# A decoder layer in float32 on one core: seven block products per weight group, in another order, in fewer PSUM banks, with weights split 1024 wide

## The chip, the cores and the metric

The kernel runs on one core of a Trainium2 chip, as one launch. The metric is the device time of that core in microseconds (us). The engines are named as the profile names them: PE (TensorE matmul), PEld (its weight loads), DVE (VectorE), ACT (ScalarE), POOL (GpSimd), SP (SyncE, which issues nearly all DMAs).

## The reference

One decoder layer on 1024 tokens of width 1024, all in float32. The two feed-forward blocks (FFN1 and FFN2, inner width 2816) are where the change lies; the mixer between them isn't touched.

```python
def swiglu(h, w_gate, w_up, w_down):
    return (jax.nn.silu(h @ w_gate) * (h @ w_up)) @ w_down

h = modulate(rms_norm(x, ffn1_norm[l]), sh1, sc1)
x = x + 0.5 * g1[:, None, :] * swiglu(h, ffn1_w_gate[l], ffn1_w_up[l], ffn1_w_down[l])
...
h = modulate(rms_norm(x, ffn2_norm[l]), sh3, sc3)
x = x + 0.5 * g3[:, None, :] * swiglu(h, ffn2_w_gate[l], ffn2_w_up[l], ffn2_w_down[l])
```

## The kernel before, in words

**Matmuls in three pieces.** Each float32 operand is split into a high part (rounded to fp32r by an ACT cast) and a low part (the rest, by a DVE subtraction). `mm3` issues three matmuls of 512 columns for one product of 128 by 128 by 512: high by high, high by low, low by high. The weights are split on the chip too: `Weights.pump` takes a raw tile of 1 MB that SP has loaded (`rawp`, two buffers), casts 512 or 1024 columns of it on ACT and subtracts on DVE, into a tile named w of 1024 columns (a granule). `ws.take()` gives the next granule to PE, `ws.free()` gives its slot back and calls `pump`, so that each split is emitted where a slot was freed. The instructions of DVE and of ACT are issued in the order in which the program emits them.

**Seven products in place of eight.** The 2816 inner columns are 11 groups of 256. In most groups (fa2 to fa10 in FFN1, fb1 to fb10 in FFN2) gate and up are each computed as a product of two-by-two blocks with seven block products instead of eight: A11, A12, A22 and the sums S1 to S4 of blocks of the activations, against B11, B12, B22 and sums of blocks of the weights (t1 to t4 in the code). One block product of one side (g for gate, u for up) is 12 matmuls into one PSUM bank. `seven(name, between, place, kept, then)` does first all seven products of g, then all seven of u. Its table names the bank of each: A11 and A12 accumulate in A, S1 and S4 in C, S2 in B, S3 in D, A22 in E. The sums over the banks are made after the products: per side one ACT copy (of A11) and five DVE additions, each of 128x512 with one operand in PSUM. The pool `mm_ps` has six banks; a new tile takes the bank that was released longest ago, and PE waits until the readers of the tile that had it are done.

**Weight sums.** Each raw tile of a seven-product group holds B11, B21, B22, B12 of gate or up, 512 columns each. `combine` (L168, L169) and `split_done` (L177, L179) form the sums with four POOL operations of 128x512 per raw tile, eight per group. A granule is two blocks that stand one after the other in the list SEVEN, so it is split in two halves of 512, and belongs to products n and n+1 of one side.

**Down projections.** `down7` does the same with seven products for four groups at a time (fad0, fad1, fbd0, fbd1), over two pairs of output tiles p; their results update x by a DVE operation. `down2` is the plain down projection of one group: 16 tiles of 6 matmuls, each followed by an update of x on DVE. For group fb0 it runs inside fb1: `seven("fb1", lambda: down2(...), 0, ...)` calls it as `between` after the first product of g. In the program's names its PSUM tiles are fb0d, with d from 0 to 7 for the two token halves.

**Around it.** In FFN1, work that the mixer needs later (names bb, cl, bl, rot, tab, ph and the like) is emitted in small steps between the matmuls by `clock.tick`. `keep`, `keep_sums` and `keep_last` store the products' results to DRAM; `fetch` brings them back for `down7`. Names in the profile: fa6gC is bank C of group fa6's gate side, fa6gt, fa6gu its SBUF tiles, h and h1S (h3 and h3S in FFN2) the split activations and their sums.

Of the kernel before, what the change touches and what calls it, by code (L numbers as in the profile page):

```python
# [13 lines left out]
F32 = mybir.dt.float32  # L14
# [3 lines left out]
ALU = mybir.AluOpType  # L18
# [102 lines left out]
class Weights:  # L121
# [5 lines left out]
    SEVEN = (0, "t1", "t2", "t3", 3, "t4", 2)  # L127
    SECOND = (0, "t2", 3, "t3", "t1", "t4", 2)

    def __init__(self, engines, srcs, granules, raw_bufs):  # L130
        self.V, self.A, self.SP, self.G = engines
        self.srcs, self.granules, self.raw_bufs = srcs, granules, raw_bufs
        self.left = [0] * len(srcs)
        self.combined = {j for pair in granules for j, c in pair if isinstance(c, str)}
        for pair in granules:
            for j, _ in pair:
                self.left[j] += 1
# [3 lines left out]
        self.slots = deque()  # L141

# [9 lines left out]
    def load(self, upto):  # L152
        while len(self.raws) < min(upto, len(self.srcs)):
# [3 lines left out]
            self.raws.append(r[:].rearrange("p a b -> p (a b)"))  # L157
# [6 lines left out]
    def combine(self, j):  # L164

        f = self.sums_pool.tile([P, HALF], F32, tag="sums", name=f"sums{j}")[:]
        r = [self.raws[j][:, c * HALF : (c + 1) * HALF] for c in range(4)]
        self.G.tensor_tensor(out=f, in0=r[2], in1=r[1], op=ALU.subtract)  # L168
        self.G.tensor_tensor(out=r[1], in0=r[1], in1=r[0], op=ALU.subtract)  # L169
        self.sums[j] = {"t1": r[1], "t2": r[0], "t3": f, "t4": r[0]}  # L170

    def split_done(self, j, c):

        if j in self.combined and c in (0, "t2"):
            s, r = self.sums[j], self.raws[j][:, :HALF]
            if c == 0:
                self.G.tensor_tensor(out=r, in0=s["t3"], in1=r, op=ALU.add)  # L177
            else:
                self.G.tensor_tensor(out=r, in0=self.chunk(j, 3), in1=r, op=ALU.subtract)  # L179

    def chunk(self, j, c):
        if isinstance(c, int):
            return self.raws[j][:, c * 512 : (c + 1) * 512]
        return self.sums[j][c]

    def pump(self):
        while self.slots and len(self.tiles) < len(self.granules):
            i = len(self.tiles)
            pair = self.granules[i]
            (j0, c0), (j1, c1) = pair  # L190
            if self.sums_pool is None and (j0 in self.combined or j1 in self.combined):
                return
            self.load(max(j0, j1) + 1)
            for j, c in pair:
                if j in self.combined and j not in self.sums:
                    self.combine(j)
# [3 lines left out]
            if j0 == j1 and isinstance(c0, int) and c1 == c0 + 1:  # L200
                parts = [(slice(0, 1024), self.raws[j0][:, c0 * 512 : (c0 + 2) * 512])]
            else:
                parts = [(slice(512 * q, 512 * q + 512), self.chunk(*c)) for q, c in enumerate(pair)]
# [6 lines left out]
            for j, _ in pair:  # L210
                self.left[j] -= 1
# [24 lines left out]
def hymba_layer(ctx: ExitStack, tc, x_d, xt_d, wm1_d, wmod_d, gu1_d, gs1_d, ds1_d, wl1_d, win_d, wout_d, glu_d, gu2_d, gs2_d, wd2_d, ds2_d, wl2_d, cols_d, cond_d, lam_d, bc_d, out_d):  # L236
# [49 lines left out]
    def plain(arrays):  # L286
        for a in arrays:
            granules.extend([[(len(srcs), 2 * q), (len(srcs), 2 * q + 1)] for q in range(2)])
            srcs.append(a)

    def stream(gu, gs, wd, ds, wl, m):
# [4 lines left out]
        for g in range(m, NGRP):  # L296
# [3 lines left out]
            seven = [(i, c) for i in (j, j + 1 + inner) for c in Weights.SEVEN]  # L300
            seven = [seven[i : i + 2] for i in range(0, 14, 2)]
            if inner:
                granules.extend(seven[:1] + [[(j + 1, 2 * q), (j + 1, 2 * q + 1)] for q in range(2)] + seven[1:])
            else:
                granules.extend(seven)
        for c in range(CHUNKS):
            for p in range(2):
                j = len(srcs)
                srcs.extend([ds[c, p, 0], ds[c, p, 1]])
                granules.extend([(j, s), (j + 1, s)] for s in Weights.SECOND)  # L310
# [338 lines left out]
    def seven(name, between, place=1, kept=None, then=None):  # L649


        a_tiles, gate_, taken = {}, {}, []

        for side in "gu":
            bank, res = {}, {}

            def add(dst, src, b):
                V.tensor_tensor(out=dst[:], in0=src[:], in1=bank[b][:], op=ALU.add)

            def out(h, fi, t):  # L660
                nm = f"{name}_{fi}_{h}"
                if side == "g":
                    A.activation(t[:], t[:], AF.Silu)
                    gate_[h, fi] = t
                elif kept is None:
                    V.tensor_tensor(out=t[:], in0=t[:], in1=gate_[h, fi][:], op=ALU.mult)
                    a_tiles[fi, h] = split_act(t[:], nm + "a")
                else:
                    keep(kept, f"A{h + 1}{fi + 1}", t[:], gate_[h, fi][:], ALU.mult, name, t[:])

            for n, (left, b) in enumerate(SEVEN):
                q = n + 7 * (side == "u")
                if q % 2 == 0:
                    taken = ws.take()
                opens = b not in bank
                if opens:
                    bank[b] = ps(f"{name}{side}{b}")
                for k in range(4):
                    while len(blocks[left]) <= k:
                        clock.step()  # L680
                    mm3(bank[b][:], taken[0], q % 2 * 4 + k, blocks[left][k], opens and k == 0, k == 3, more=not opens)
                nm = f"{name}{side}"
                if n == 0:
                    t1 = t2k(nm + "t1")
                    A.copy(t1[:], bank["A"][:])
                elif n == 2:
                    u2 = t2k(nm + "u2")
                    add(u2, t1, "B")
                elif n == 3:
                    u3 = t2k(nm + "u3")  # L690
                    add(u3, u2, "D")
                    add(t1, u3, "C")
                    out(1, 1, t1)
                elif n == 4 and side == "g":
                    t = pools["first"].tile([P, HALF], F32, tag="first", name=nm + "c11") if "first" in pools else acc_in_mov(nm + "c11")
                    A.activation(t[:], bank["A"][:], AF.Silu)
                    gate_[0, 0] = t
                elif n == 4:
                    t = gate_[0, 0]
                    if kept is None:  # L700
                        V.tensor_tensor(out=t[:], in0=t[:], in1=bank["A"][:], op=ALU.mult)
                        a_tiles[0, 0] = split_act(t[:], f"{name}_0_0a")
# [1196 lines left out]
```

## Time and profile before

| | |
|---|---|
| runs (us) | 1698.07, 1703.12, 1702.21; median 1702.21 |
| profiled execution: its span (the page gives no other time for it) | 1704.7 us, 20844 instructions |
| busy share of the span | PE 98%, DVE 74%, ACT 37%, POOL 22% |
| instructions | PE 7545 matmuls, DVE 1957, ACT 1064, POOL 297 |

The stages by the trace: a start up to 34 us; plain groups fa0 and fa1 up to 119.87; seven-product groups fa2 to fa10 up to about 460; down projections to 765; the mixer to 985; its output projection to 1055; FFN2 (fb0, fb1 to fb10, fbd0, fbd1 and a last plain down projection) to the end. A row of the trace's timeline gives start, duration, engine, line, operation, out<-in by name, count, and in brackets the idle time before it with what ended it. A helper records most operations, so that nearly all have line L112; the names tell them apart.

### The profile page before, as it was taken

To read this page: it belongs to the slowest core of one execution; us is meant where nothing else is said; L and a number is where in the kernel's file an instruction comes from. 1 tells how busy PE (TensorE), PEld (TensorE's weight loads), DVE (VectorE), ACT (ScalarE), POOL (GpSimd) and SP (SyncE) were. 2 spreads that over 40 slices of the span, in tenths; PEclk is the share of its full clock that TensorE was granted. 3 is DMA by queue.
4 is the path that set the end of the run, shared out by engine and by line. 5 is a ranking of instruction groups with operands and counts; after the bars stand their busy time and mean duration, and the time that the engine had idled before them with its cause. 6 is when DMAs were issued, how large, how long until landed. Compare 5 with 4: busy or idle time off the path is not lost.

```text
span 1704.7 us, 20844 instructions
## 1 busy us (share of the span) xinstructions
PE 1666.8 (98%) x7545; PEld 1369.9 (80%) x7545; DVE 1255.5 (74%) x1957; ACT 630.1 (37%) x1064; POOL 382.0 (22%) x297
## 2 busy tenths in 40 slices
PE   8999999999999999999999999999999999999997
PEld 5888877788878888788777878888888888888886
DVE  7897899998589978735555857957767667576655
ACT  6525323333354332331113415434344434322233
POOL 1012222242222412100000021122333223333212
PEclk9999999999999999999999999999999999999999
DMA  8544454544665448244654232324443343759212
GB/s 350 187 148 137 172 189 155 183 149 139 213 216 170 151 152 291 70 111 149 191 151 134 70 129 112 112 74 182 188 174 148 148 173 148 269 228 381 110 50 99
DMA packets 101625, 281.48 MB, mean 165 GB/s; under 512 B 19345, under 2 KB 34961, under 8 KB 90386
## 3 DMA queue, kind: packets, MB, share of 16 engines
q1 hardware_dynamic: 101522, 280.15, 46.6%
q8 instruction: 59, 0.97, 0.2%
q14 instruction: 44, 0.36, 0.1%
HBM read 195.69 MB, written 76.02 MB: 159 GB/s over the span
## 4 chain that ended last, share of the span: by engine, by line
PE 70%; DVE 8%; DMA 5%; issue 1%; ACT 0%; SPq 0%; POOL 0%; DVEq 0%; ACTq 0%; POOLq 0%
PE wo L112 4%; PE fald L112 3%; PE fb10d L112 2%; PE u L112 2%; PE fbd_1B L112 2%; PE fbd_0B L112 2%; DMA swz<-si 2%; DVE w L112 2%; PE fad_1B L112 2%; PE b L112 2%; PE fad_0B L112 1%; PE c L112 1%; PE fb0u L112 1%; PE fad_1C L112 1%; PE fbd_1C L112 1%; PE fbd_0C L112 1%
## 5 line engine op out<-in xcount | busy, mean ns | idle before, releaser
L112 ACT CAST w<-raw 128x512 fp32r<-128x512 f32 (+1 forms) x374 | 240.9, 677 | 497.7 <-issue 72.7
L112 DVE TENSOR_TENSOR w<-raw,w 128x512 fp32r<-128x512 f32 (+1 forms) x374 | 311.2, 851 | 101.2 <-ACT w L112 100.6
L177 POOL TENSOR_TENSOR raw<-sums,raw 128x512 f32<-128x512 f32 x54 | 81.6, 1511 | 420.9 <-DVE w L112 419.9
L168 POOL TENSOR_TENSOR sums<-raw 128x512 f32<-128x512 f32 x54 | 76.4, 1415 | 308.1 <-DMA raw<-in_ds 129.1
L179 POOL TENSOR_TENSOR raw<-raw 128x512 f32<-128x512 f32 x54 | 82.3, 1526 | 86.6 <-DVE w L112 86.0
L112 DVE CUSTOM_DVE_ANT_0 wm<-wm,cact 128x1024 f32<-128x1024 f32 x56 | 77.7, 1407 | 15.1 <-DMA wm<-in_wmod 15.0
L169 POOL TENSOR_TENSOR raw<-raw 128x512 f32<-128x512 f32 x54 | 85.2, 1577 | 4.2
L370 POOL TENSOR_TENSOR n3aq<-n3aq,n3aq 128x512 f32<-128x512 f32 x5 | 7.5, 1499 | 277.4 <-ACT n3aq L112 277.2
L112 DVE TENSOR_TENSOR w<-sums,w 128x512 fp32r<-128x512 f32 x54 | 54.9, 1029 | 3.4 <-ACT w L112 2.8
L112 PE MATMUL p<-h,w 128*128 128x512 f32 x192 | 49.4, 407 | 2.0 <-ACT h L112 1.5
L112 PE MATMUL wo<-oa,w 128*128 128x512 f32 x192 | 45.5, 391 | 2.1 <-ACT w L112 1.3
L112 PE MATMUL c<-h,w 128*128 128x512 f32 x192 | 47.1, 397 | 0.0
L112 PE MATMUL v<-h,w 128*128 128x512 f32 x192 | 46.9, 395 | 0.0
L112 PE MATMUL b<-h,w 128*128 128x512 f32 x192 | 45.6, 393 | 0.0
L112 PE MATMUL wo<-ob,w 128*128 128x512 f32 x192 | 45.2, 391 | 0.0
L112 PE MATMUL u<-h,w 128*128 128x512 f32 x192 | 44.8, 392 | 0.2 <-DVE h L112 0.2
L112 PEld LDWEIGHTS wo<-oa,w 128*128 128x128 f32 x192 | 35.8, 188 | 10.2 <-ACT w L112 1.7
L112 PEld LDWEIGHTS p<-h,w 128*128 128x128 f32 x192 | 35.7, 192 | 10.1 <-ACT h L112 2.0
L112 ACT CAST w<-sums 128x512 fp32r<-128x512 f32 x54 | 32.7, 619 | 28.8 <-PE fa10gE L112 2.5
L112 PEld LDWEIGHTS u<-h,w 128*128 128x128 f32 x192 | 35.7, 188 | 8.3 <-DVE h L112 0.6
L112 PEld LDWEIGHTS wo<-ob,w 128*128 128x128 f32 x192 | 35.8, 188 | 7.4
L112 PEld LDWEIGHTS c<-h,w 128*128 128x128 f32 x192 | 35.8, 190 | 7.2
(1579 smaller groups left out, 4039.8 us busy)
## 6 DMA issues: line engine op xcount, KB each, us to landing
raw<-in_gs SPq DMA_DIRECT2D x38, 1024.0 KB, 5.0
wm<-in_wmod SPq DMA_DIRECT2D x56, 512.0 KB, 5.2
raw<-in_ds SPq DMA_DIRECT2D x16, 1024.0 KB, 6.6
mw<-in_wm SPq DMA_DIRECT2D x8, 1024.0 KB, 8.4
raw<-in_win SPq DMA_DIRECT2D x8, 1024.0 KB, 5.5
raw<-in_gu SPq DMA_DIRECT2D x6, 1024.0 KB, 4.9
raw<-in_wl SPq DMA_DIRECT2D x5, 1024.0 KB, 6.7
xb<-in_xt SPq DMA_DIRECT2D x8, 512.0 KB, 6.4
```

The costliest lines, as they stand in the source:

```text
L112: r = getattr(self.engine, name)(*args, **kw)
L168: self.G.tensor_tensor(out=f, in0=r[2], in1=r[1], op=ALU.subtract)
L169: self.G.tensor_tensor(out=r[1], in0=r[1], in1=r[0], op=ALU.subtract)
L177: self.G.tensor_tensor(out=r, in0=s["t3"], in1=r, op=ALU.add)
L179: self.G.tensor_tensor(out=r, in0=self.chunk(j, 3), in1=r, op=ALU.subtract)
L370: nc.gpsimd.tensor_tensor(out=a, in0=a, in1=sq[:, :n], op=ALU.add)
```

## The change

The raw tiles are laid out otherwise by the host: of each group, raw tile j holds B11 and B12, raw tile k = j+1 holds B22 and B21, each block with its 512 gate columns and its 512 up columns side by side. A granule is now one block for gate and up, split by one ACT cast and one DVE subtraction of 1024 columns; seven granules a group, as before. POOL forms the sums with four operations of 128x1024 per group (L170, L171, L172 of the new kernel one after the other, once both raw tiles are there, and L191 after the granule t3 is split). The pool of sums has one buffer of 1024 columns in place of two of 512.

`seven` does each product for g and then for u. The order is now A11, S1, S2, A12, S3, S4, A22, and the banks are B, C, B, A, B, C, B: the products in B accumulate on one another and are read in between. Per side there are three ACT copies (t1, c1, u2) and three DVE additions; the last product is read straight from bank B. `between` runs after the first product of both sides, `then` (fetches for the next `down7`) once per product of both sides, and the storing of sums comes after the whole group. `down7` uses the same table.

```diff
+    def seven(j, k):
+        return [(j, 0, k), (j, "t1", k), (j, "t2", k), (k, 1, k), (j, "t3", k), (k, 0, k), (j, "t4", k)]
...
+    def chunk(self, j, c, k):
         if isinstance(c, int):
+            return self.raws[j][:, c, :]
+        if c == "t1":
+            f = self.sums[j] = self.sums_pool.tile([P, 1024], F32, tag="sums", name=f"sums{j}")
+            b11, b12, b22 = self.raws[j][:, 0, :], self.raws[j][:, 1, :], self.raws[k][:, 0, :]
+            self.G.tensor_tensor(out=f[:], in0=b22, in1=b12, op=ALU.subtract)
+            self.G.tensor_tensor(out=b12, in0=b12, in1=b11, op=ALU.subtract)
+            self.G.tensor_tensor(out=b11, in0=f[:], in1=b11, op=ALU.add)
+        return {"t1": self.raws[j][:, 1, :], "t2": self.raws[j][:, 0, :]}.get(c, self.sums[j][:])
...
-            for q, src in parts:
-                hi, lo = w[:, 0, q], w[:, 1, q]
-                self.A.copy(hi, src)
-                self.V.tensor_tensor(out=lo, in0=src, in1=hi.bitcast(F32), op=ALU.subtract)
-                self.split_done(*pair[q.start // HALF])
+            hi, lo = w[:, 0, :], w[:, 1, :]
+            self.A.copy(hi, src)
+            self.V.tensor_tensor(out=lo, in0=src, in1=hi.bitcast(F32), op=ALU.subtract)
+            if c == "t3":
+                f = self.sums[j][:]
+                self.G.tensor_tensor(out=f, in0=self.raws[k][:, 1, :], in1=self.raws[j][:, 0, :], op=ALU.subtract)
...
-    SEVEN = (("A11", "A"), ("S1", "C"), ("S2", "B"), ("S3", "D"), ("A12", "A"), ("A22", "E"), ("S4", "C"))
-    SECOND = (("A11", "A"), ("S2", "B"), ("A12", "A"), ("S3", "B"), ("S1", "C"), ("A22", "B"), ("S4", "C"))
+    SEVEN = (("A11", "B"), ("S1", "C"), ("S2", "B"), ("A12", "A"), ("S3", "B"), ("S4", "C"), ("A22", "B"))
...
+        for n, (left, b) in enumerate(SEVEN):
+            (w,) = ws.take()
+            for half, side in enumerate("gu"):
...
+                    mm3(bank[b, side][:], w, 4 * half + k, blocks[left][k], opens and k == 0, k == 3, more=not opens)
                 if n == 0:
+                    copied(t1, "B", side, "t1")
+                elif n == 1:
+                    copied(c1, "C", side, "c1")
                 elif n == 2:
+                    copied(u2, "B", side, "u2")
                 elif n == 3:
+                    add(t1, "A", side)
+                    out(side, 0, 0, t1[side], t1[side])
                 elif n == 4:
+                    add(c1, "B", side)
+                    out(side, 1, 1, c1[side], c1[side])
                 elif n == 5:
+                    add(u2, "C", side)
+                    out(side, 0, 1, u2[side], u2[side])
+                else:
+                    if side == "g":
+                        last = pools["first"].tile([P, HALF], F32, tag="first", name=f"{name}c21") if "first" in pools else acc_in_mov(f"{name}c21")
+                    out(side, 1, 0, bank["B", side], last)
+            ws.free()
+            if n == 0 and between is not None:
+                between()
+            if then is not None:
+                then(left)
...
-        ws.sums_pool = es.enter_context(tc.tile_pool(name="sums", bufs=2))
+        ws.sums_pool = es.enter_context(tc.tile_pool(name="sums", bufs=1))
...
-    seven("fb1", lambda: down2(a_prev, 2, "fb0", (0, 1)), 0, kept[1])
+    seven("fb1", lambda: down2(a_prev, 2, "fb0", (0, 1)), kept[1])
```

How the order of the instructions moves is shown at two places. The first is DVE in the middle of group fa6; w is a granule's low part, X a stored sum, bb, cl, clt and bl belong to the mixer's preparation. Before:

```order
L112 TENSOR_TENSOR bl_2812<-tab_1652,bb_2764 128x512
L112 TENSOR_TENSOR fa6uu_2778<-fa6ut_2704,fa6uB 128x512
L112 TENSOR_TENSOR w_2783<-raw_2573,w_2783 128x512 x2
L112 TENSOR_TENSOR fa6uu_2802<-fa6uu_2778,fa6uD 128x512
L112 TENSOR_TENSOR fa6ut_2704<-fa6uu_2802,fa6uC 128x512
L112 TENSOR_TENSOR fa6X<-fa6ut_2704,fa6gt_2523 128x512
L112 TENSOR_TENSOR fa6X<-fa6gc_2644,fa6uA 128x512
```

Changed:

```order
L112 TENSOR_TENSOR fa6gc_2496<-fa6gc_2496,fa6gB 128x512
L112 TENSOR_TENSOR bb_2655<-prm_2652,qq 128x128
L112 TENSOR_TENSOR bb_2656<-prm_2652,qq 128x128
L112 TENSOR_TENSOR bb_2654<-bb_2655,bb_2656 128x64 x2
L112 TENSOR_TENSOR cl_2661<-tab_1609,prm_2652 128x576
L112 TENSOR_TENSOR clt_2662<-tab_1610,prm_2652 128x576
L112 TENSOR_TENSOR fa6uc_2511<-fa6uc_2511,fa6uB 128x512
L112 TENSOR_TENSOR cl_2661<-cl_2661,clt_2662 128x576
L112 TENSOR_TENSOR fa6X<-fa6uc_2511,fa6gc_2496 128x512
L112 TENSOR_TENSOR w_2671<-raw_2517,w_2671 128x1024
```

Before, bank C is given back only by the second of two additions that stand behind the product S3 of the same side; in the change one addition stands behind each product, and bank B of g is given back by fa6gc's.

The second place is DVE in `down2` of group fb0, inside fb1; the rows x<-fb0d are the updates that give fb0d's banks back, h3S are pieces of split activations, w the splits for fb1's next products. Before:

```order
L112 SCALAR_TENSOR_TENSOR x_0_3915<-fb0d_0_8957,gate,x_0_3915 128x512
L112 SCALAR_TENSOR_TENSOR x_0_3915<-fb0d_0_8969,gate,x_0_3915 128x512
L112 TENSOR_TENSOR h3S_0_8944<-h3S_0_8944 128x512
L112 SCALAR_TENSOR_TENSOR x_1_3918<-fb0d_1_8977,gate,x_1_3918 128x512
L112 TENSOR_TENSOR h3S_1_8964<-h3S_1_8964 128x512
L112 TENSOR_TENSOR h3S_2_8984<-h3S_2_8984 128x512
L112 SCALAR_TENSOR_TENSOR x_1_3918<-fb0d_1_8989,gate,x_1_3918 128x512
L112 TENSOR_TENSOR h3S_3_9004<-h3S_3_9004 128x512
L112 SCALAR_TENSOR_TENSOR x_1_3919<-fb0d_1_8997,gate,x_1_3919 128x512
L112 SCALAR_TENSOR_TENSOR x_1_3919<-fb0d_1_9009,gate,x_1_3919 128x512
L112 TENSOR_TENSOR w_9017<-raw_8442,w_9017 128x512
L112 TENSOR_TENSOR w_9017<-sums_8713,w_9017 128x512
```

Changed:

```order
L112 SCALAR_TENSOR_TENSOR x_0_3723<-fb0d_0_8686,gate,x_0_3723 128x512
L112 TENSOR_TENSOR h3S_0_8655<-h3S_0_8655 128x512
L112 SCALAR_TENSOR_TENSOR x_0_3724<-fb0d_0_8694,gate,x_0_3724 128x512
L112 TENSOR_TENSOR h3S_1_8681<-h3S_1_8681 128x512
L112 TENSOR_TENSOR w_8671<-raw_8159,w_8671 128x1024
L112 TENSOR_TENSOR h3S_2_8701<-h3S_2_8701 128x512
L112 SCALAR_TENSOR_TENSOR x_0_3724<-fb0d_0_8706,gate,x_0_3724 128x512
L112 TENSOR_TENSOR h3S_3_8721<-h3S_3_8721 128x512
L112 SCALAR_TENSOR_TENSOR x_1_3727<-fb0d_1_8714,gate,x_1_3727 128x512
```

The split of the granule t1 (w_8671) stood behind the eighth update and stands now between the third and the fourth. In the built program fb0d's tiles take five PSUM banks in turn before (fb1's bank A of g holds the sixth), and four in the change (fb1's bank B of g and of u hold two): the fourth tile's bank is written again by the ninth tile before, and by the eighth in the change.

## Rows read from the trace of the kernel before

**Rows 1.** The page, part 1: busy time, share of the span, instructions.
```profile
PE 1666.8 (98%) x7545; PEld 1369.9 (80%) x7545; DVE 1255.5 (74%) x1957; ACT 630.1 (37%) x1064; POOL 382.0 (22%) x297
```
**Rows 2.** Busy time by stage: length, each engine (instructions), granted clock, DMA share, GB/s.
```profile
90.00:140.00 50.00, 49.07 (x217) 40.34 (x216) 45.82 (x108) 19.75 (x32) 12.71 (x41) 1.00 0.36 122
140.00:450.00 310.00, 305.62 (x1384) 249.11 (x1383) 262.19 (x399) 105.33 (x194) 92.28 (x61) 1.00 0.49 166
450.00:640.00 190.00, 186.43 (x818) 152.70 (x817) 159.73 (x219) 83.98 (x148) 52.37 (x34) 1.00 0.52 178
...
1055.00:1643.00 588.00, 588.00 (x2597) 486.88 (x2596) 416.62 (x587) 218.42 (x380) 162.76 (x110) 1.00 0.46 176
```
**Rows 3.** What PE waited for, 90 to 700 us: total, times, longest.
```profile
PE fa4gC L112 <- DVE fa4gt L112: 1.6, 1, 1.6
PE fa10uC L112 <- DVE fa10ut L112: 1.5, 1, 1.5
PE fad_0A L112 <- DVE w L112: 1.5, 2, 0.8
PE fa5gC L112 <- DVE fa5gt L112: 1.2, 1, 1.2
PE fa2gC L112 <- DVE fa2gt L112: 0.9, 1, 0.9
PE fa5uC L112 <- DVE fa5ut L112: 0.9, 1, 0.9
PE fa6gC L112 <- DVE fa6gt L112: 0.7, 1, 0.7
PE fad_0B L112 <- DVE fad_0u L112: 0.5, 1, 0.5
```
**Rows 4.** Timeline of PE in group fa6: two products in a row.
```profile
315.30 2.88 PE L112 MATMUL fa6uA<-h,w 128*128 128x512 f32 x12
318.02 2.88 PE L112 MATMUL fa6uE<-h,w 128*128 128x512 f32 x12
```
**Rows 5.** Groups by shape on DVE: busy, mean ns of one, idle before, releaser.
```profile
L112 DVE TENSOR_TENSOR w<-raw,w 128x512 fp32r<-128x512 f32 x324 | 249.2, 791 | 67.4 <-ACT w L112 67.0
L112 DVE TENSOR_TENSOR w<-raw,w 128x1024 fp32r<-128x1024 f32 x50 | 62.0, 1244 | 33.8 <-ACT w L112 33.6
```
**Rows 6.** Groups by shape on ACT: a granule's casts, and the copy of a bank.
```profile
L112 ACT CAST w<-raw 128x512 fp32r<-128x512 f32 x324 | 188.5, 619 | 376.5 <-issue 72.7 <-POOL raw L177 60.7 <-DMA raw<-in_ds 44.1
L112 ACT CAST w<-raw 128x1024 fp32r<-128x1024 f32 x50 | 52.3, 1049 | 121.2 <-PE v L112 31.0 <-PE fald L112 18.4 <-PE wo L112 15.0
L112 ACT COPY fa3gt<-fa3gA 128x512 f32<-128x512 f32 x1 | 0.6, 589 | 1.6 <-PE fa3gA L112 1.6
```
**Rows 7.** Timeline of POOL in group fa6.
```profile
318.37 1.62 POOL L169 TENSOR_TENSOR raw<-raw 128x512 f32<-128x512 f32 x1
319.96 1.27 POOL L177 TENSOR_TENSOR raw<-sums,raw 128x512 f32<-128x512 f32 x1
```
**Rows 8.** Timeline of DVE in the same stretch.
```profile
318.76 0.68 DVE L112 TENSOR_TENSOR fa6uu<-fa6uu,fa6uD 128x512 f32<-128x512 f32 x1
319.47 0.69 DVE L112 TENSOR_TENSOR fa6ut<-fa6uu,fa6uC 128x512 f32<-128x512 f32 x1
320.19 1.59 DVE L112 TENSOR_TENSOR fa6X<-fa6ut,fa6gt 128x512 f32<-128x512 f32 x1
```
**Rows 9.** Timeline of PE at the start of group fb1.
```profile
1088.32 2.88 PE L112 MATMUL fb1gA<-h,w 128*128 128x512 f32 x12
1091.04 5.60 PE L112 MATMUL fb0d<-fb_0a,w 128*128 128x512 f32 x24
1096.48 5.60 PE L112 MATMUL fb0d<-fb_1a,w 128*128 128x512 f32 x24
```
**Rows 10.** Timeline of POOL at the same place.
```profile
1096.51 1.30 POOL L168 TENSOR_TENSOR sums<-raw 128x512 f32<-128x512 f32 x1 [18.14 <-DMA raw<-in_gs]
1097.88 1.29 POOL L169 TENSOR_TENSOR raw<-raw 128x512 f32<-128x512 f32 x1
```
**Rows 11.** Timeline of DVE at the same place.
```profile
1102.77 1.40 DVE L112 SCALAR_TENSOR_TENSOR x<-fb0d,gate,x 128x512 f32<-128x512 f32 x2
1104.09 0.68 DVE L112 TENSOR_TENSOR w<-raw,w 128x512 fp32r<-128x512 f32 x1
```
**Rows 12.** Timeline of ACT in group fa2: first and last of 13 rows without a gap.
```profile
137.33 1.17 ACT L112 COPY rt<-ph 64x512 f32<-64x512 f32 x1
...
146.54 1.14 ACT L112 CAST w<-raw 128x512 fp32r<-128x512 f32 x2
```

More of the change, by code (lines that the diff above doesn't have):

```diff
@@ L133, in __init__ @@
         self.left = [0] * len(srcs)
[L134 to L137, printed above, removed]
+        for j, c, _ in granules:
+            self.left[j] += c != "t4"
         self.raws, self.tiles, self.sums, self.kinds = [], [], {}, []
@@ L188, in pump @@
             i = len(self.tiles)
-            pair = self.granules[i]
-            (j0, c0), (j1, c1) = pair
-            if self.sums_pool is None and (j0 in self.combined or j1 in self.combined):
+            j, c, k = self.granules[i]
+            if self.sums_pool is None and c == "t1":
                 return
[L193 to L196, printed above, removed]
+            self.load((k if c == "t1" else j) + 1)
+            src = self.chunk(j, c, k)
             pool = self.slots.popleft()
@@ L287, in plain @@
         for a in arrays:
-            granules.extend([[(len(srcs), 2 * q), (len(srcs), 2 * q + 1)] for q in range(2)])
+            granules.extend((len(srcs), q, None) for q in range(2))
             srcs.append(a)
@@ L644, in combos3 @@
             yield
-    SEVEN = (("A11", "A"), ("S1", "C"), ("S2", "B"), ("S3", "D"), ("A12", "A"), ("A22", "E"), ("S4", "C"))
-    SECOND = (("A11", "A"), ("S2", "B"), ("A12", "A"), ("S3", "B"), ("S1", "C"), ("A22", "B"), ("S4", "C"))
[L649 to L675, printed above, removed]
@@ L686, in seven @@
                 elif n == 2:
-                    u2 = t2k(nm + "u2")
-                    add(u2, t1, "B")
+                    copied(u2, "B", side, "u2")
                 elif n == 3:
[L690 to L697, printed above, removed]
-                elif n == 4:
[L699 to L702, printed above, removed]
-                    else:
-                        keep(kept, "A11", t[:], bank["A"][:], ALU.mult, name, t[:])
-                elif n == 5:
-                    add(u3, u3, "E")
-                    out(1, 0, u3)
-                    if side == "u" and kept is not None and kept.sums:
-                        keep_sums(kept, name)
-                elif n == 6:
-                    add(u2, u2, "C")
-                    out(0, 1, u2)
-                    if side == "u" and kept is not None and kept.sums:
-                        keep_last(kept, name)
@@ L721, in seven @@
+            ws.free()
[3 more added lines that the diff above has]
+                then(left)
+        if kept is not None and kept.sums:
+            keep_sums(kept, name)
+            keep_last(kept, name)
         return a_tiles
@@ L1432, in hymba_layer @@
             pools.pop("first")
-        seven(f"fa{g}", lambda: None, kept=kept[g], then=(lambda left: fetch_chunk(0, left)) if g == NGRP - 1 else None)
+        seven(f"fa{g}", kept=kept[g], then=(lambda left: fetch_chunk(0, left)) if g == NGRP - 1 else None)
     down7("fad0", lefts[0], 0, lambda left: fetch_chunk(1, left), lambda left: load_x(range(2), (1, 3)) if left == "A12" else None)
```

120 lines of the change are left out of this document (50 added, 70 removed).

## The prediction

> **What bounds the kernel now.** I read the busy shares first [rows 1]: PE is busy for 1666.8 of 1704.7 us, and the reader is to see that nothing else comes near: DVE 74%, ACT 37%, POOL 22%. The change issues the same matmuls, so work saved on DVE, ACT or POOL is worth only what PE waits for them. So the second view is busy time by stage, where PE's idle time is the stage's length less its PE time [rows 2]: 0.9 us in 90 to 140, 4.4 in 140 to 450, 3.6 in 450 to 640, nothing at all in 1055 to 1643, where FFN2's seven-product groups lie. The granted clock is 1.00 in all four, the 2.4 GHz level, so no clock is to be won there. The third view is what PE waited for [rows 3]. Eight entries, 8.8 us in all, which is the idle time of the three stages. This is the ceiling of the gain: 0.5% of the span.
>
> Six entries, 6.8 us, are of one kind: the product S4 wants to open bank C again, and the second DVE addition behind S3 hasn't yet read it. The other two, 2.0 us, lie in the down projection fad0: a weight split that came late, and one addition.
>
> The sum is made against the profiled execution, 1704.7 us; it lies 2.5 us above the median of the runs, 1702.2, and I carry the difference over to the median.
>
> **The engines beside PE.** Of DVE's additions, 76 go in the 19 groups (two per side) and 32 in the down projections: 108 at 0.68 us [rows 8], about 73 us. 378 splits of 512 become 189 of 1024, at 1.24 us each [rows 5] in place of two at 0.79 or more; some 65 us. ACT gets 108 copies at 0.59, 64 us, and 189 casts at 1.05 in place of 378 at 0.62, 36 us less [rows 6]. POOL does 108 operations of twice the size, for about the same time. I count all of this at nothing: it lies beside matmuls, and DVE, the fullest, had 262 us of 310 filled in its worst stage [rows 2]. If that cover were gone it would show as waits, which are counted below.
>
> **The waits at bank C: gone.** A product of one side lasts 318.02 − 315.30 = 2.72 us [rows 4]. Before, S1 lies in C until the second addition behind S3; S4 is three products later, A12 and A22 lie between, so the additions have 2 × 2.72 = 5.4 us, behind splits and mixer work in DVE's order. In the change the shortest time that a bank has to be read is three products, 8.2 us: B of g after A11 (A11 of u and both S1 lie between), the same after S2, and after S3. Two of the three reads are ACT copies, and ACT is 34% busy there; the third is a single addition. A late read as in [rows 3], up to 1.6 us after 5.4, would end at 7.0, inside 8.2. So the five entries at fa4, fa5, fa6 and fa10, 5.9 us, go. What is late next are the granules: a slot comes free two products of both sides before it is used, 4 × 2.72 = 10.9 us, and cast and split take 2.3 of that [rows 5, 6].
>
> **fa2.** Its 0.9 us goes too, but ACT runs there without a gap from 137.33 to 147.68 on the mixer's tables [rows 12], and in the change the copies of S2 stand in the midst of that, with S3's matmuls due at 119.87 + 8 × 2.72 = 141.6. Adding up ACT's rows in the new order I get a copy between just in time and 1.5 us late. I take **0.6 us** new (ends 0 and 1.5).
>
> **fad0.** 28 pieces that were fetched for it are subtracted by DVE, in order, between the additions; before, it cost 2.0 us. With three additions and three copies per output in place of five and one, its margins by the order are 1 to 2 us. I take **0.8 us** left (ends 0 and 3).
>
> **fb1: a new wait.** Here the change moves work past a queue. Before, group fb1's first sums needed one raw tile. In the change t1 and t2 need both raw tiles of the group, and with two raw buffers the second is loaded only after the down weights of fb0 are split. That tile lands at 1096.51, where POOL starts today too [rows 10]. Then come L170 and L171, each twice the 1.30 us of a 512-wide one: to about 1101.7, or 1102.3 with one subtraction of DVE between them. ACT casts to 1103.4. The split, w_8671, stands in DVE's order ahead of the update of fb0d's fourth tile. And here a row of another place decides: an operation of DVE with two SBUF inputs that meets one of POOL waits until that one ends. In group fa6 it started at 320.19, POOL's ran to 319.96 + 1.27 = 321.23, and it took 1.59 us in place of 0.68 [rows 7, 8]; the additions from PSUM beside L169 kept their 0.68. So the split waits for L172, which starts as L171 ends: 1104.9 plus 1.2 for itself, 0.6 for an h3S piece, 0.7 for the update [rows 11]: 1107.4. When is the bank wanted? fb0d starts after two products, 1088.32 + 5.44 = 1093.76, a tile takes (1096.48 − 1091.04)/4 = 1.36 us [rows 9], and with four banks the eighth tile, due at 1093.76 + 7 × 1.36 = 1103.3, writes the fourth's. PE waits **4.1 us**. If POOL didn't hold the split, it would end at 1104.0 from a cast at 1102.8, and PE would wait about 2.1; the ends are 0 (the raw tile or the update earlier than I think) and 5.5 (one more operation held). Today the same split came at 1104.09, behind the eighth update, and PE waited for nothing.
>
> The Trainium skill says the same of the hold (SBUF — State Buffer, section "SBUF: two separate sides"): POOL and a DVE operation with two SBUF inputs take a shared pair of ports as an exclusive lock for the whole instruction. By a shared bandwidth instead, the wait at fb1 would be the 2.1 us, the sum 2 us lower; the trace agrees with the lock, 1.59 against 0.68 us.
>
> **The sum.** −8.8 + 0.6 + 0.8 + 4.1 = −3.3 us. From 1702.2: **1698.9 us**, which is 0.2% and inside the 0.3% (5.1 us) that a measurement of this kernel can tell from no change.
>
> **The rivals.**
>
> *Faster, 1694.* The waits at bank C go and fb1's doesn't come, because the raw tile lands earlier or the update isn't held: −8.8 + 0.6 + 0.8 = −7.4, so 1694.8; with a wait of 1 us, 1695.8. For it: fb1's bound from below is 0, and FFN2 has no wait today. Against it: each link of fb1's chain is a row. Chance 0.33, fb1 waits of up to 2.2 us included.
>
> *No gain.* The change does to the banks what it says, but DVE stays late: a DVE that is 85% full with splits twice as long meets S3's addition late, and 3 to 5 us of waits come back at bank B in fa3 to fa10. Net 0 to +2, 1702 to 1704. For it: DVE's share in that stage; against it: four additions and seven splits fewer per group, and a lateness of 1.6 us at most today. With the forecast itself this makes the 0.53 of "same" (forecast alone 0.40).
>
> *Slower, 1708 and more.* POOL's three wide sums in a row hold DVE. Today POOL's operations are 1.3 us and come two at a time [rows 7, 10]; in the change L170, L171 and L172 are 2.6 each and follow one another, 7.8 us in which DVE gets through one SBUF operation after each. In fa2 to fa10 the addition behind S3 has cl, clt and bb operations ahead of it in the order; if three of them are held for 2.6 us each, 7.8 of the slack of 8.2 is gone, and the addition itself needs 0.7. It decides at an average lateness of 0.9 us: nine groups of 0.9 us make +8.4 with the sum above, so +5.1; at 1.5 us, +10.2, and 1712. For it: the hold in [rows 8]. Against it: by the new order the sums of the next group come when its second raw tile has landed, mostly after S3 of g. The rule of the skill named above gives this case as well: a lock held for each whole instruction makes DVE's delay grow with POOL's width; the trace has shown it at 1.27 us, and no run here yet at 2.6. Chance 0.14.
>
> **How the numbers follow.** Forecast and "no gain" are within 0.3%: 0.53. Faster by over 0.3%: 0.33. Slower by over 0.3%: 0.14. The range of the forecast's own terms: fb1 from 0 to 5.5, fa2 to 1.5, fad0 to 3, gives −8.8 to +1.2, 1693.4 to 1703.4; with 1.5 us for the runs' own spread below, and the nearer half of the slower case above, 1692.0 to 1706.5.
>
> **What would show it.** Right: instruction counts of DVE near 1660, ACT 983, POOL 189; no entry for bank C or B of fa3 to fa10 among PE's waits; an entry of fb0d of about 4 us with the split w before an update of x, and idle PE time of about that in 1055 to 1643, where there was none. Wrong: an fb0d entry under 1 us (then 1695), or entries of fa gB and uB that repeat from group to group behind long DVE rows beside L170 to L172 (then over 1705). Several small waits in fb2 to fb10 would be a cause that I haven't priced.

## The result and the profile after

The changed kernel takes 1707.45 us in the median of 17 runs (1701.88 to 1713.3), the kernel before 1702.91 of 17 (1698.07 to 1707.01): ratio 1.0031, 95% interval 1.0021 to 1.0042. It is slower, by 4.5 us. The prediction said 1698.9 and no change. On another chip the same kernel gave 1706.97 and 1.0019 (1.0006 to 1.0032).

The profiled execution is one of 1708.08 us, with a span of 1706.2. Its busy shares, part 1 of the page, answer to [rows 1]:

```profile
PE 1668.5 (98%) x7545; PEld 1373.4 (80%) x7545; DVE 1188.2 (70%) x1660; ACT 667.8 (39%) x983; POOL 341.2 (20%) x189
```

The counts are those forecast, and DVE does 67 us less. PE's idle time over the whole span, 37.7 us, is that of before, 37.9. By stage (against [rows 2]):

```profile
90.00:140.00 50.00, 50.00 (x222) 41.39 (x221) 43.43 (x106) 18.21 (x23) 9.38 (x36) 1.00 0.28 95
140.00:450.00 310.00, 305.90 (x1373) 249.55 (x1372) 245.18 (x312) 117.36 (x176) 83.84 (x32) 0.99 0.50 172
450.00:640.00 190.00, 189.59 (x836) 156.70 (x836) 153.90 (x173) 90.25 (x134) 46.73 (x17) 1.00 0.52 183
...
1055.00:1643.00 588.00, 584.75 (x2573) 483.67 (x2572) 376.37 (x428) 236.68 (x333) 143.33 (x56) 1.00 0.45 175
```

The stages with fa2 and with fad0 gained 0.9 and 3.2 us of PE time. In 140 to 450, where the waits at bank C were to go, PE idles 4.1 us in place of 4.4, and the granted clock has fallen to 0.99. FFN2, without a wait before, idles 3.3 us. The waits of PE in these stages (against [rows 3]):

```profile
PE fb0d L112 <- DVE x L112: 3.3, 1, 3.3
...
PE fa5gB L112 <- DVE fa5gc L112: 1.9, 1, 1.9
PE fa6uB L112 <- DVE fa6uc L112: 1.9, 1, 1.9
...
PE fad_0C L112 <- DVE w L112: 0.4, 1, 0.4
PE kp L112 <- DVE bl L112: 0.3, 1, 0.3
```

Eight waits of 8.8 us in all, the longest 1.6, have become five of 7.8 us, three of them longer than any before. (kp is a matmul of the mixer's preparation, which waited for nothing before.) By their lengths alone the kernel should be 1 us faster. What they cost more stands in the timeline of PE around the wait in fa5:

```profile
272.13 4.29 PE L112 MATMUL fa5gB<-h,w 128*128 128x512 f32 x12 [1.91 <-DVE fa5gc L112]
276.22 3.24 PE L112 MATMUL fa5uB<-h,w 128*128 128x512 f32 x12
279.30 2.88 PE L112 MATMUL fa6gB<-h,w 128*128 128x512 f32 x12
```

From start to start the first product behind the wait takes 4.09 us and the second 3.08, in place of 2.72 each [rows 4]: 1.7 us lost with PE busy. The granted clock of the wait and of the stretch behind it, at fa5, fa6 and fb0d (columns as in [rows 2]):

```profile
270.10:272.10 2.00, 0.13 (x1) 0.00 (x0) 1.97 (x4) 0.08 (x1) 0.89 (x1) 1.00 0.05 11
272.90:276.30 3.40, 3.40 (x11) 2.62 (x10) 3.40 (x6) 0.69 (x1) 0.00 (x0) 0.59 0.14 31
...
320.70:324.10 3.40, 3.40 (x11) 2.64 (x10) 3.40 (x5) 0.81 (x2) 1.30 (x1) 0.59 0.51 190
...
1102.40:1105.80 3.40, 3.40 (x10) 2.67 (x10) 3.08 (x6) 1.04 (x1) 0.00 (x0) 0.58 0.00 0
```

The wait itself still shows 1.00; behind each of the three long waits PE runs near the lower of its two levels, 1.2 GHz. So they cost 7.1 us of idle time and 5.2 us of slow matmuls, 12.3 us, where before no wait in these stages had a slow stretch behind it (the clock is 1.00 in all of [rows 2]).

The two spans are nevertheless only 1.5 us apart. The mixer, which the change doesn't touch, has slow stretches of its own, and they differ from one execution to the next: worked out from the granted clock in 765 to 985, its matmuls lost 4.6 us in the profile of before, 3.1 in this one and nothing in the second profile of the changed kernel. What the change costs is therefore read from the medians, and the two profiles show where.

**The wait at fb0d** is the one forecast. DVE and POOL at the place, two answers of the timeline:

```profile
1098.11 2.75 DVE L112 TENSOR_TENSOR w<-raw,w 128x1024 fp32r<-128x1024 f32 x1 [0.57 <-ACT w L112]
1100.78 0.68 DVE L112 TENSOR_TENSOR h3S<-h3S 128x512 fp32r<-128x512 f32 x1
1101.39 0.74 DVE L112 SCALAR_TENSOR_TENSOR x<-fb0d,gate,x 128x512 f32<-128x512 f32 x1
```
```profile
1097.07 2.71 POOL L172 TENSOR_TENSOR raw<-sums,raw 128x1024 f32<-128x1024 f32 x1
```

The split waits until L172 ends at 1099.8, takes 2.75 us, and the fourth update follows: PE waits 3.25 us.

**The waits at fa5 and fa6** were not in the forecast. DVE, POOL and SP ahead of the wait at fa5, where the addition fa5gc gives bank B back:

```profile
266.39 2.22 DVE L112 TENSOR_TENSOR dg<-ident,lam 16x64 f32<-16x64 f32 x1 [2.84 <-DMA si_d<-rot]
268.70 2.36 DVE L112 TENSOR_TENSOR kc<-kc,dg 16x64 f32<-16x64 f32 x1
271.10 0.29 DVE L112 TENSOR_TENSOR bb<-prm,qq 128x128 f32<-128x128 f32 x1
271.31 0.68 DVE L112 TENSOR_TENSOR fa5gc<-fa5gc,fa5gB 128x512 f32<-128x512 f32 x1
```
```profile
266.15 2.39 POOL L170 TENSOR_TENSOR sums<-raw,raw 128x1024 f32<-128x1024 f32 x1 [10.40 <-DMA raw<-in_gs]
268.62 2.37 POOL L171 TENSOR_TENSOR raw<-raw 128x1024 f32<-128x1024 f32 x1
```
```profile
255.78 0.33 SPq L112 DMA_DIRECT2D raw<-in_gs  x1
...
260.20 0.55 SPq L112 DMA_DIRECT2D raw<-in_gs  x1
260.80 0.95 SPq L112 DMA_DIRECT2D si_d<-rot  x1
261.84 0.55 SPq L112 DMA_DIRECT2D si_d<-rott  x1
```

DVE idles 2.84 us for si_d, a store of 128 KB of the mixer's preparation (a raw tile is 1 MB). Then POOL starts, and two operations of 16x64, 0.21 us each elsewhere, are held for 2.2 and 2.4 us. The addition is done at 272.0; PE wanted the bank at 270.2. On SP the second raw tile now goes out 4.4 us behind the first and right ahead of that store. Before, at the same place, the second stood behind the stores, 13.7 us after the first (the same view of the kernel before; no wait of DVE for si_d in 140 to 450 is over 0.6 us there):

```profile
254.54 0.34 SPq L112 DMA_DIRECT2D raw<-in_gs  x1
265.64 0.60 SPq L112 DMA_DIRECT2D si_d<-rot  x1
266.35 0.54 SPq L112 DMA_DIRECT2D si_d<-rott  x1
268.19 0.33 SPq L112 DMA_DIRECT2D raw<-in_gs  x1
```

At fa6 the chain has the same form behind another transfer. DVE waits 3.54 us, by the profile for the store mk_d; L170 starts at 312.98; and two pairs of bb operations, 0.6 and 0.4 us per pair at fa5, are held ahead of the addition fa6uc:

```profile
313.34 2.39 DVE L112 TENSOR_TENSOR bb<-prm,qq 128x128 f32<-128x128 f32 x2 [3.54 <-DMA mk_d<-kc]
315.76 2.44 DVE L112 TENSOR_TENSOR bb<-bb,bb 128x64 f32<-128x64 f32 x2
```

### The profile page after: what moved, and what is told of

It reads as the page before. It is cut to its first block, busy times and chain, and to the rows that moved or that the text cites. A ratio compares the mean times of both kernels' runs of the same rounds, so it can differ in the third digit from the quotient of the medians.

```text
span 1706.2 us, 20362 instructions
## 1 busy us (share of the span) xinstructions
PE 1668.5 (98%) x7545; PEld 1373.4 (80%) x7545; DVE 1188.2 (70%) x1660; ACT 667.8 (39%) x983; POOL 341.2 (20%) x189
## 4 chain that ended last, share of the span: by engine, by line
PE 68%; DVE 7%; DMA 4%; issue 1%; POOL 1%; ACT 1%; SPq 0%; DVEq 0%; POOLq 0%; ACTq 0%
PE wo L112 4%; PE fald L112 3%; PE fbd_1B L112 3%; PE fbd_0B L112 3%; PE fb10d L112 2%; PE u L112 2%; PE fad_1B L112 2%; PE fad_0B L112 2%; DMA swz<-si 2%; PE b L112 2%; DVE w L112 1%; PE fbd_1C L112 1%; PE fbd_0C L112 1%; PE c L112 1%; PE fad_1C L112 1%; PE fad_0C L112 1%
## 5 line engine op out<-in xcount | busy, mean ns | idle before, releaser
L112 DVE TENSOR_TENSOR w<-raw,w 128x1024 fp32r<-128x1024 f32 x185 | 244.9, 1325 | 158.4 <-ACT w L112 158.0
L112 ACT CAST w<-raw 128x1024 fp32r<-128x1024 f32 x185 | 194.1, 1050 | 263.7 <-PE v L112 35.0
L191 POOL TENSOR_TENSOR sums<-raw,raw 128x1024 f32<-128x1024 f32 x27 | 66.6, 2468 | 481.3 <-DVE w L112 481.3
L170 POOL TENSOR_TENSOR sums<-raw,raw 128x1024 f32<-128x1024 f32 x27 | 70.0, 2594 | 355.5 <-DMA raw<-in_gs 128.5
L112 DVE TENSOR_TENSOR w<-sums,w 128x1024 fp32r<-128x1024 f32 x54 | 66.0, 1222 | 71.6 <-ACT w L112 71.6
L172 POOL TENSOR_TENSOR raw<-sums,raw 128x1024 f32<-128x1024 f32 x27 | 71.9, 2661 | 51.3 <-DVE w L112 50.8
L171 POOL TENSOR_TENSOR raw<-raw 128x1024 f32<-128x1024 f32 x27 | 73.7, 2731 | 2.1
L112 ACT CAST w<-sums 128x1024 fp32r<-128x1024 f32 x54 | 56.7, 1050 | 43.6 <-PE fbd_1A L112 15.8
```

The costliest lines, as they stand in the source:

```text
L112: r = getattr(self.engine, name)(*args, **kw)
L170: self.G.tensor_tensor(out=f[:], in0=b22, in1=b12, op=ALU.subtract)
L171: self.G.tensor_tensor(out=b12, in0=b12, in1=b11, op=ALU.subtract)
L172: self.G.tensor_tensor(out=b11, in0=f[:], in1=b11, op=ALU.add)
L191: self.G.tensor_tensor(out=f, in0=self.raws[k][:, 1, :], in1=self.raws[j][:, 0, :], op=ALU.subtract)
```

## The experiments

Ratios are to runs of the kernel before on the same chip, with 95% intervals. The changed kernel itself came out at 1.0031 and at 1.0019, so a saving of 2 or 3 us against it is not more than a hint. Two theories for the loss were on the table at first: the order on DVE ahead of the reads that free a bank, and the hold by POOL's wide operations; the transfers came third.

**The price of a wait** (kernel before with waits added).

```diff
                     u3 = t2k(nm + "u3")
+                    for _ in range(dict(fb3g=5, fb4g=6, fb5g=7, fb6g=8, fb7g=10).get(nm, 0)):
+                        V.tensor_tensor(out=u3[:], in0=u2[:], in1=u2[:], op=ALU.add)
                     add(u3, u2, "D")
```

> The kernel before with 5, 6, 7, 8 and 10 extra DVE additions (0.6 us each) ahead of the read of bank D in the gate side of fb3 to fb7, where PE waits for nothing; this measures the price of a PE wait by itself. Theory (a wait costs its own length, and a long one half-clock matmuls behind it as well): PE waits at fb3gC to fb7gC that grow by 0.6 us per addition, from about 1 to about 4 us; the matmuls behind the short ones keep their 0.227 us, behind the long ones stand 3.4 us at clock 0.5 each, 1.7 us lost. Rival (the dips of the clock come at times of their own): dips as in the kernel before, none behind the five waits.

1723.91 us (2 runs), ratio 1.0120 (1.0096 to 1.0144). PE's timeline, each wait with the product behind it and the next:

```profile
1196.23 3.00 PE L112 MATMUL fb3gC<-h3S,w 128*128 128x512 f32 x12 [1.09 <-DVE fb3gt L112]
1199.07 2.88 PE L112 MATMUL fb3uA<-h,w 128*128 128x512 f32 x12
...
1237.27 3.01 PE L112 MATMUL fb4gC<-h3S,w 128*128 128x512 f32 x12 [2.46 <-DVE fb4gt L112]
1240.12 2.66 PE L112 MATMUL fb4uA<-h,w 128*128 128x512 f32 x11
...
1279.78 4.61 PE L112 MATMUL fb5gC<-h3S,w 128*128 128x512 f32 x12 [3.46 <-DVE fb5gt L112]
1284.23 2.01 PE L112 MATMUL fb5uA<-h,w 128*128 128x512 f32 x8
...
1324.92 4.61 PE L112 MATMUL fb6gC<-h3S,w 128*128 128x512 f32 x12 [4.46 <-DVE fb6gt L112]
1329.37 1.31 PE L112 MATMUL fb6uA<-h,w 128*128 128x512 f32 x5
```

Behind 1.09 and 2.46 us the product takes 2.84; behind 3.46 and 4.46 it takes 4.45, which is 1.7 us more. Behind the wait in fb7, 4.65 us, the loss is 2.2 us. The theory holds: these slow stretches come behind long waits, at places where the kernel before has none. The length alone doesn't settle it, since at fa5 and fa6 of the changed kernel 1.9 us were enough, and here 2.46 were not.

**The order in fb1.** Split of t1 behind the eighth update:

```diff
-            ws.free()
             if n == 0 and between is not None:
                 between()
+            ws.free()
...
+                    ws.behind = r if name == "fb0" and dh == 0 else None
...
+            if self.behind is not None:
+                self.V.follow(r, self.behind)
```

> Only the place of one split changes: in fb1 the granule t1 (and what follows it) is split behind the eighth update of x in fb0d, as in the kernel before, and not between the third and the fourth. Theory (few long waits, each followed by a stretch at half clock): the changed kernel's 3.3 us wait at fb0d goes, and with it the 3.4 us at clock 0.5 that follows it (1.7 us of work lost), so about 5 us less than the changed kernel: 1702 to 1703 against 1707.45, no PE wait in 1055 to 1643. Rival (the wait only moves to t1's own product S1, or the time lost lies in the mixer and in DMA): 1706 or more, with a new PE wait at fb1gC.

1704.93 us, 1.0013 (1.0002 to 1.0024). The fb0d wait is 1.4 us, with no slow stretch behind it; 2.5 us of the 5 expected came (1 to 3 by the ratios). The same split behind the twelfth update (the `free` of the first half of the down weights moved behind the first half of the second):

> The changed kernel with fb1's t1 split behind the twelfth update of x, and nothing else; the raw tiles loaded as in the changed kernel. Theory: fb0d under 2 us with no half-clock stretch behind it, the waits at fa5gB and fa6uB as in the changed kernel; 1703 to 1705.5, with the wide spread of the changed kernel's runs. Rival (fb1 is most of it): 1700 to 1702.

1705.06 us, 1.0010 (0.9996 to 1.0023): as expected, with fa5gB at 2.0, fa6uB at 1.5 and fb0d at 1.4. That last wait isn't the split's any more: h3S pieces, held by POOL, stand ahead of the fifth update.

**The hold.** Each POOL sum in two halves:

```diff
-            self.G.tensor_tensor(out=f[:], in0=b22, in1=b12, op=ALU.subtract)
+            for q in (slice(0, HALF), slice(HALF, 1024)):
+                self.G.tensor_tensor(out=f[:, q], in0=b22[:, q], in1=b12[:, q], op=ALU.subtract)
...
```

> Each of the four POOL sums of 128x1024 is issued as two of 128x512; all else as in the changed kernel. Theory of the hold (a DVE operation with two SBUF inputs waits for the whole POOL operation that it meets): DVE's longest small operations in fa5 and fa6 fall from 2.2 to 2.4 us to about 1.3 to 1.5, the waits fa5gB and fa6uB of 1.9 us fall below 1 us or go, the half-clock stretches behind them too: 3 to 6 us less, 1702 to 1704; the fb0d wait falls from 3.3 to about 2.5. Rival (what is late there is the DMA that DVE waits for in order, and the hold adds nothing): the same two waits within 0.5 us, 1706 to 1708.

1704.72 us, 1.0012 (1.0001 to 1.0024): 2.7 us less. fa6uB fell to 0.3, but fa5gB stood at 2.3 and fb0d at 3.7. DVE at fa5:

```profile
268.60 1.15 DVE L112 TENSOR_TENSOR dg<-ident,lam 16x64 f32<-16x64 f32 x1 [4.58 <-DMA si_d<-rot]
```

dg and kc are held for 1.15 us each in place of 2.2 and 2.4, beside POOL operations of about 1.27 us; but DVE had waited 4.58 us for the store, in place of 2.84. Half right: the hold follows the width of POOL's operations, and something ahead of it counts too.

**The mixer's steps behind the additions.** Two tries. In the first, steps are held back during every product:

```diff
-        if self.since >= self.period:
...
+        if self.since >= self.period and not self.held:
...
+                clock.held = True
                 for k in range(4):
```

> In the seven-product groups a step of the mixer's preparation is emitted only behind the evacuation of the product that was running, not within its matmuls; all else as in the changed kernel, the wide POOL sums too. Theory (the addition behind S3 stands in DVE's order behind a step that waits for a DMA and is then held by POOL): fa5gB and fa6uB go or fall under 0.5 us with their half-clock stretches, about 7 us of the profiled execution, 1701 to 1704 in the median, the fb0d wait of 3.3 us stays. Rival (DVE is simply too full while POOL runs): other B or C entries of 1 to 2 us in fa3 to fa10, 1706 to 1709.

1713.51 us, 1.0062 (1.0048 to 1.0077). fa5gB and fa6uB were gone, yet the kernel was 6 us slower: the program's step counter (its class `Clock`) has a cap that drops what a held step is late, so that the steps left over all came in fa10, and their stores stood on SP ahead of fad0's weights:

```profile
PE fad_0C L115 <- ACT w L115: 8.0, 1, 8.0
```

(With the fb1 edit added it gave 1711.49, where about 1698.5 was expected.) The second try holds them during S3 alone and drops none:

> The run that moved the mixer's steps, mended: the steps are held back only while product S3 of both sides runs, and none is dropped (there they were dropped by the clock's cap, so that they were all emitted in fa10, ahead of fad0's weights on SP); all else as in the changed kernel, the wide POOL sums and fb1 too. Theory (order on DVE ahead of the addition behind S3): fa5gB and fa6uB under 0.5 us, fad_0C back to 0.4 to 1.2, fb0d still 3 to 4 us: 2.5 to 5 us less than the changed kernel, 1702.5 to 1705. Rival (a full DVE, whatever the order): B or C entries of 1 to 2 us elsewhere in fa3 to fa10, 1706 to 1709.

1705.25 us, 1.0013 (0.9999 to 1.0027), just above what was expected; no fa bank among the waits, fb0d 3.3, and kp 1.9. All three edits together:

> Three edits on the changed kernel: split of t1 behind the eighth update in fb1, POOL sums in halves, steps held back during S3. Theory: all new waits but those at fad0 (about 1 us) and fb0d (under 1 us) go and with them the half-clock stretches at fa5 and fb1: 1707.45 - 2.5 - 2.7 - 2 = about 1700, a little below the kernel before (1702.1 to 1702.9). Rival (the savings are not additive, or the change costs something outside these waits): 1702 or more although no wait over 1 us is left in the seven-product stages.

1703.32 us, 0.9996 (0.9984 to 1.0008), not the 1700 expected, and a row that shows what was wrong with the theory, PE in fa6:

```profile
284.72 1.86 PE L115 MATMUL kp<-cl,bl 128*16 128x128 f32 x8 [4.77 <-DVE bl L115]
```

DVE's dg had waited 4.17 us for the store si_d there. Moving the steps moves the wait to kp, which PE must issue in order. The mended form (steps one at a time, twelfth update) and its twin with wide sums:

> The run with all three edits, two of them mended: fb1's t1 is split behind the twelfth update of x, not the eighth (the fb0d wait that was left, 1.4 to 1.9 us), and the held steps of the mixer come out one at a time, three mm3 calls apart (the wait of kp's matmuls for bl, 4.8 us, came from two at once). POOL sums in halves. Theory (what is lost lies in these waits and the half-clock stretches behind them): no PE wait over 1.2 us between 90 and 1640 us, 1698 to 1701, faster than the kernel before by 0.1 to 0.3%. Rival (the change costs about as much outside these waits as it saves): 1702 to 1704, no faster than before, with the waits gone.

> As the run with all three edits mended, but with the wide POOL sums of 128x1024. Theory (with the order on DVE mended the hold by a wide POOL operation delays nothing that PE waits for): within 1 us of the other run. Rival (the hold itself costs, through the splits and the h3S pieces): 2 to 3 us more, with waits at fa bank B or at kp.

1702.42 us, 0.9993 (0.9978 to 1.0008), and 1701.66, 0.9992 (0.9976 to 1.0007). kp still waited 5.2 and 5.8 us in the profiles, and the forecast of 1698 to 1701 was missed; the cause lay ahead of DVE. With the order mended, halves and wide sums can't be told apart.

**The changed kernel again**, unedited:

> The changed kernel itself, unedited, on the same chip as the two others, for a second profile of it. Theory: waits again at fb0d (3 to 4 us) and at B of one to three of the groups fa3 to fa9 (1.5 to 2.6 us each), half-clock stretches behind most of them; 1706 to 1708, 5 to 8 us above the mended one. Rival (the waits of the one profile were chance): a profile without the fa waits, and the same median.

1706.97 us. This profile has fb0d 3.2, fa6uB 2.1, fa5gB 1.0, kp 1.9; against the expectation only the first of these has a slow stretch behind it (PE's timeline shows one other, in 714 to 720). The mean granted clock of its 12 runs is 0.9917, of the 29 runs of before on the same chip 0.9936: 0.0019 of 1703 us is 3.2 us, and the means differ by 3.5. By this estimate nearly all of what the change loses is time at the lower level, and the waits' own lengths cancel. (The clock is that of the whole span, the mixer included.)

**The second raw tile's load.** First far too late:

```diff
-            self.ahead()
+            if not (7 <= (k or 0) <= 17 and (j == k or c == "t4")):
+                self.ahead()
...
+            if i in range(9, 20, 2):
+                self.SP.follow(dma, last)
```

> The changed kernel with one edit: for fa4 to fa9 the load of a group's second raw tile is issued some 11 us after the first, not 4 to 5, and behind the mixer's small stores on SP; product order, POOL and DVE as in the changed kernel. Theory (two 1 MB loads in a row make the small transfers late that DVE waits for, in order, ahead of the addition behind S3): DVE's waits for si_d and mk_d in 140 to 450 fall from 2.8 and 3.5 us to under 1.5 us, fa5gB, fa6uB and kp waits under 1 us each, and 2 to 4 us less than the changed kernel (1707): 1703 to 1705. Rival (those transfers are late for another reason, or the sums now come too late): the same waits, or waits for DVE w in fa4 to fa9; 1706 or more.

1720.75 us, 1.0118 (1.0098 to 1.0137). DVE's waits for the stores and PE's at bank B and kp are gone, as the theory wanted, and the rival came as well: t1's sums are late, and the product S1 waits.

```profile
204.51 0.73 PE L112 MATMUL fa4gC<-h1S,w 128*128 128x512 f32 x2 [2.25 <-ACT w L112]
206.95 4.63 PE L112 MATMUL fa4gC<-h1S,w 128*128 128x512 f32 x10 [1.71 <-DVE w L112]
```

(With the fb1 edit, 1716.49, where about 1701 was expected.) Then one granule earlier, the condition cut to `7 <= (k or 0) <= 17 and j == k`, alone and with the fb1 edit:

> The changed kernel with the second raw tile of fa4 to fa9 loaded behind the mixer's small stores, and nothing else; fb1 as in the changed kernel. Theory (most of what was lost lies in FFN1's waits, which differ from run to run, with the half-clock stretches behind them): no fa B entry over 1 us, the fb0d wait of 3 to 4 us stays; 1700 to 1703, with a spread of the runs of some 4 us in place of 11. Rival (fb1 is most of it): 1704 to 1706.

> Changed kernel with fb1's t1 split behind the twelfth update, and the second raw tile of fa4 to fa9 loaded one granule earlier than in the run where it came 11 us late: behind the mixer's small stores, some 6 to 8 us after the first tile. Theory (the load in front of the small stores makes DVE late): no wait of PE over 1 us at fa banks or at kp, and none for the splits of S1; 1699 to 1702, at or below the kernel before. Rival (the sums are late again): waits at fa4gC to fa7gC for w of 1 to 2 us, 1705 to 1710; or the same fa B and kp waits as without it, 1703 to 1705.

> The same with the POOL sums in halves of 512. Theory: what is left of the hold goes, 0 to 1.5 us less than with the wide sums. Rival (halves make no difference once the order is right, or cost POOL time ahead of t1): 0 to 1.5 us more.

Alone: 1701.80 us, 0.9993 (0.9981 to 1.0004), 5 us below the changed kernel, with fb0d at 3.3, kp at 1.6 and no fa bank among PE's waits; its 12 runs spread over 7 us, where 4 were expected. With fb1's split behind the twelfth update as well: **1696.60 us** (1694.86 to 1697.74, 6 runs), 0.9963 (0.9949 to 0.9976), below what was expected, faster than both kernels and over 10 us below the changed one. With halves on top, 1697.81, 0.9971 (0.9961 to 0.9982): no gain. The place in fa5 in the run of 1696.60 us, SP, DVE and POOL:

```profile
261.18 1.42 SPq L112 DMA_DIRECT2D si_d<-rot  x1
262.69 0.54 SPq L112 DMA_DIRECT2D si_d<-rott  x1
263.33 0.54 SPq L112 DMA_DIRECT2D raw<-in_gs  x1
```
```profile
265.04 0.21 DVE L112 TENSOR_TENSOR dg<-ident,lam 16x64 f32<-16x64 f32 x1 [0.46 <-DMA si_d<-rott]
...
265.83 0.68 DVE L112 TENSOR_TENSOR fa5gc<-fa5gc,fa5gB 128x512 f32<-128x512 f32 x1
```
```profile
268.73 2.56 POOL L173 TENSOR_TENSOR sums<-raw,raw 128x1024 f32<-128x1024 f32 x1 [11.96 <-DMA mk_d<-kc]
```

The store goes first, dg waits 0.46 us, POOL starts 2.6 us later and meets neither dg nor kc, and the addition starts at 265.83, not 271.31. (The order of DVE moved a little with the load: a bb operation now stands ahead of kc. That this plays no part was not tested by itself.)

The waits' lengths and the clock together also give the other runs, as an estimate: the change in PE's waits of the profile against the 8.8 us of before (in 90 to 700 and 1055 to 1643), and the difference of the mean clocks of the runs times 1703 us. For the load and fb1's split together −5.6 and −0.7 us, measured −6.2; for the load alone −3.9 and +2.4, measured −1.0; for fb1's split behind the twelfth update −0.9 and +3.6, measured +2.3.

## Why the prediction was wrong

*What bounds the kernel, and the ceiling.* Right: PE, and the old waits at bank C are gone in every run with the new order.

*fa2, fad0.* 0.6 and 0.8 us were forecast; the profile has 0 and 0.4, the second profile 0.2 and 0. Small, and less than forecast.

*fb1.* Right in its mechanism: forecast 4.1 us idle, measured 3.25, the split held by L172 and the fourth update behind it. The whole place came some 4.5 us earlier than assumed, POOL's start (1091.78 for 1096.51) and fb0d's (1089.25 for 1093.76) alike, so that it cancels. But the wait's price was 5.0, with the slow matmuls behind it.

*"The waits at bank C: gone."* This step failed. The old waits at C went, but it put the waits at bank B at nothing, and two of 1.9 us came. It let a late read of up to 1.6 us pass inside 8.2 us and argued from DVE's and ACT's load; at fa5 the read was over 10 us behind the end of S3. It left out SP: the change moves the second raw tile's load from behind the mixer's small stores to ahead of them, since both raw tiles are now freed one product apart and are both needed for t1. DVE then waits in order, 2.84 us for a store at fa5 and 3.54 us at fa6, and POOL's sums begin at about the same time and hold what follows. The run that puts this load back behind the stores, in fa4 to fa9, removes both waits and some 5 us.

*The rival "slower"* named the hold by L170 to L172 ahead of the addition behind S3. The rows of fa5 show it for L170 and L171, and it came in two of nine groups, not as a lateness in all; the transfer in front was missed. (Its nine groups of 0.9 us are 8.1 us, not 8.4, and its turning point +4.8, not +5.1.) The Trainium skill's rule on the shared port pair (SBUF — State Buffer, section "SBUF: two separate sides"), a lock held for the whole instruction, fits here too: 16x64 operations of 0.21 us lasted 2.2 and 2.4 us beside operations of 2.4 us.

*The sum.* This step failed as well: it priced a wait at its length. The runs show 1.7 us more behind the long ones; the prediction spoke of the clock only to say that nothing was to be won there. With 1.7 us behind fb1's wait its −3.3 would have been −1.6, still no loss; the waits at fa5 and fa6, 3.8 us and 3.5 us behind them, turn the sign. With every term as the profile has it the sum is −8.8 + 7.8 + 5.2 = +4.2 us, against +4.5 measured. That this comes so near is in part luck, since each side is one execution. (The sum was made against 1704.7 us as 2.5 above the median. That is a span; in the runs listed the time is 1.7 to 1.9 us longer than the span, so that the execution lay some 4 us above the median. The forecast's difference doesn't hang on it.)

Left open: why 1.9 us were followed by a slow stretch in one profile and 2.1 or 2.46 us in others were not; and how much of the delay at fa5 and fa6 is the late transfer and how much the hold, since the load that is put back moves both. The fb1 and FFN1 edits bring 2 and 5 us alone and 10 together; by their intervals that may still be a sum.

## What to carry to other kernels

Where a change makes one tile wait for two loads, look at what the second load now stands ahead of on its queue, and who waits for that in order; the busy shares of the engines didn't show it here. Price a PE wait with the clock behind it: here a few long waits cost more than many short ones of the same sum. When moving work off an in-order queue only moves the wait, look further up.

## What was not expected of the hardware

Each PE wait of 3.2 to 5.8 us in the seven-product stages that was looked at was followed by matmuls near 1.2 GHz, worth 1.5 to 2.2 us. Behind waits of 1.7 to 2.6 us this came only sometimes. One short wait shows the chance in it best: ahead of the mixer PE waits 1.0 us and runs eight matmuls of one column, n2bst, in all 18 profiles of this case. In eight of them the ten matmuls behind it take 3.6 to 4.1 us, in ten of them, those of both kernels above included, 2.5 to 2.6. The second profile of the changed kernel:

```profile
714.44 1.05 PE L112 MATMUL n2bst<-one,n2bq 128*128 128x1 f32 x8 [0.98 <-DVE n2bq L112]
715.35 4.13 PE L112 MATMUL u<-h,w 128*128 128x512 f32 x10
```

Much of the runs' spread goes with this: in the changed kernel's 17 runs the mean granted clock lies between 0.987 (1713.3 us) and 0.994 (1702.8 us), and time and clock go together with a correlation of −0.9. On the other chip it is −0.8, and in the 29 runs of before there −0.5, so that the clock isn't all of it.
